# The first two contraction slices of a fused matmul–GELU–matmul, loaded and turned one at a time

## The chip, the core and the metric

The kernel runs on one core of one Trainium2 chip. The core has TensorE (PE in the profile; its weight loads are a row of their own, PEld), VectorE (DVE), ScalarE (ACT), GpSimd (POOL) and SyncE (SP), and 16 DMA engines that move data between the chip's main memory and the core's own. The metric is the device time of one execution in microseconds (us): the median over executions without the profiler.

## What is computed

```python
def setup_inputs():
    m, k, n, p = 1024, 1024, 2048, 1024
    return {
        "a": np.random.randn(m, k).astype(np.float32),
        "b": np.random.randn(k, n).astype(np.float32),
        "c": np.random.randn(n, p).astype(np.float32),
    }

def reference(a, b, c):
    h = np.matmul(a, b)
    h = 0.5 * h * (1 + np.tanh(np.sqrt(2 / np.pi) * (h + 0.044715 * h ** 3)))
    return np.matmul(h, c).astype(np.float32)
```

All inputs and the output are fp32 in main memory.

## The kernel before

The first product contracts over k = 1024, that is over eight slices of 128 (KT = 8). TensorE takes the contraction along the partitions, so b's slices can be used as they lie, while a must be turned: each 128 x 128 piece of a is cast to bf16, transposed on TensorE into PSUM (L145), and copied by VectorE into `aT` (L146). `aT[:, h, k]` holds slice k of row half h, where h = 0 stands for rows 0 to 511 of a and h = 1 for rows 512 to 1023.

**Stage 1** (L229 to L287) computes the first 512 columns of a·b in the plain way, in bf16. The output lies turned: column tile t (128 columns, t = 0 to 3) by row half h, each in a PSUM bank of its own `ps[h, t]`, summed over the eight slices by `block(h, tiles, ks)`, which issues one 128x128 by 128x512 matmul for each tile and slice (L114). GELU on ScalarE moves a finished bank to `hT` (L118).

**Later stages** compute the other 1536 columns of a·b and then the product with c by seven products in place of eight (class `Seven`, function `seven`; all their matmuls are at L212). VectorE makes the sums and differences that they need. They use the right half of b (`b1[:, :, 512:]`, `b2`) and `c_sb`. The change doesn't touch them.

**The loads have two routes.**

- *Plain loads* on SyncE's queue bring fp32 as it is. They go to `sta` (a) and `stb` (b), and VectorE or ScalarE cast them to bf16 (L110, L108). L75 to L79 issue, in this order: a's rows h = 0, columns 0 to 255 (512 KB); b's slices 0 and 1 of the left 512 columns (512 KB); a's h = 1, columns 0 to 255 (512 KB); a's h = 0, columns 256 to 511 (512 KB); b's slice 2 (256 KB).
- *Casting loads* on GpSimd's queue write bf16 straight into `abq`, `b1`, `b2` and `c_sb`. A part `a_part(h, q)` of a is 512 rows by 256 columns, two slices, 512 KB; q runs from 0 to 3. L91 and L92 issue a's (1, 1) and b's slice 3. The loop at L93 then issues for q = 2 and 3: a's (0, q), b's slices 2q and 2q+1, a's (1, q). Behind these follow the right half of b (L98, L101) and c (L104).

The casting queue is held back by `gate` (L81), a copy on GpSimd that reads one column of a's first plain load: GpSimd issues no casting load before that load has landed.

**The order of the work** is written out by hand. Each engine runs its own instructions in the order of the program, and waits at each for what it needs. TensorE's order in stage 1 is the text of L229 to L285. `stir` puts in small matmuls on a constant, which keep TensorE busy while it waits for the first data. `turn(h, q, i, ab)` is a generator: each `next` transposes one slice of part (h, q), four pieces, into a PSUM bank i and copies it out; from L255 on it takes its input straight from `abq`. `cast_a(h, q, ...)` casts a part with the engines named, `cast_b(k, ...)` a slice of b.

The banks matter in one place: tile t of row half 1 uses bank 4 + t, for t = 0 to 2 (L246), and the transposes of the casting parts use bank 7.

Of the kernel before, what the change touches and what calls it, by code (L numbers as in the profile page):

```python
# [9 lines left out]
F32 = mybir.dt.float32  # L10
F32R = mybir.dt.float32r
BF16 = mybir.dt.bfloat16
# [7 lines left out]
def kernel(ctx, tc, a, b, c, out):  # L20
    nc = tc.nc
    M, K = a.shape
    _, N = b.shape
    _, P = c.shape
    H = 512
# [3 lines left out]
    av = a.rearrange("(mt p) k -> p mt k", p=128)  # L29
    bv = b.rearrange("(kt p) n -> p kt n", p=128)  # L30
# [9 lines left out]
    def slot(tag, shape, dt, name):  # L40
        return big.tile(shape, dt, name=name, tag=tag)

    def bank(i, shape=(128, H), dt=F32, name="ps"):
        return pp.tile(list(shape), dt, name=name, tag=f"bank{i}", padded_shape=None)

    def pieces(tag, bufs, shape, dt, name):
        return small.tile(shape, dt, name=name, tag=tag, bufs=bufs)

    warm = nc.const_aps.tensor(0.0, [128, 256], F32)
    ident = consts.tile([128, 128], BF16, name="ident")  # L50
    make_identity(nc, ident)
    gate = consts.tile([128, 1], F32, name="gate")
# [6 lines left out]
    aT = slot("a", [128, 2, KT, H], BF16, "aT")  # L59
    b1 = slot("b1", [128, KT, 1024], BF16, "b1")  # L60
# [2 lines left out]

    KH = KT // 2
    stb = slot("x0", [128, KT, H], F32, "stb")
    sta = slot("x1", [128, 2, 2, 4, 256], F32, "sta")
    abq = slot("x3", [128, 4, 2, 4, 256], BF16, "abq")

    def a_part(h, q):
        return av[:, 4 * h:4 * h + 4, ds(q * 256, 256)]  # L70

    def b_part(q):
        return bv[:, 2 * q:2 * q + 2, 0:H]

    nc.sync.dma_start(out=sta[:, 0, 0], in_=a_part(0, 0))  # L75
    nc.sync.dma_start(out=stb[:, 0:2], in_=b_part(0))
    nc.sync.dma_start(out=sta[:, 1, 0], in_=a_part(1, 0))
    nc.sync.dma_start(out=sta[:, 0, 1], in_=a_part(0, 1))
    nc.sync.dma_start(out=stb[:, 2], in_=bv[:, 2, 0:H])  # L79

    nc.gpsimd.tensor_copy(gate, sta[:, 0, 0, 3, 0:1])  # L81
    nc.scalar.activation(g, warm[:, 0:1], AF.Gelu_apprx_tanh)


    def cast_load_a(h, q):
        nc.gpsimd.dma_start(out=abq[:, q, h], in_=a_part(h, q))  # L86

    def cast_load_b(q):
        nc.gpsimd.dma_start(out=b1[:, 2 * q:2 * q + 2, 0:H], in_=b_part(q))  # L89

    cast_load_a(1, 1)  # L91
    nc.gpsimd.dma_start(out=b1[:, 3, 0:H], in_=bv[:, 3, 0:H])  # L92
    for q in range(2, 4):  # L93
# [5 lines left out]
    for n in range(2):  # L99
        for k in range(0, KT, 4):  # L100
            nc.gpsimd.dma_start(out=b2[:, k:k + 4, ts(n, H)],  # L101
                                in_=bv[:, k:k + 4, ds(1024 + n * H, H)])
# [3 lines left out]
    def copy(eng, dst, src):  # L106
        if eng is nc.scalar:
            nc.scalar.activation(dst, src, AF.Copy)  # L108
        else:
            nc.vector.tensor_copy(dst, src)  # L110

    def mm1(p, t, h, ks):
        for k in ks:
            nc.tensor.matmul(p, b1[:, k, ts(t, 128)], aT[:, h, k],  # L114
                             start=(k == 0), stop=(k == KT - 1))
# [6 lines left out]
    def stir(*widths):  # L122

        for w in widths:
            nc.tensor.matmul(ps[0, 3][:, 0:w], warm[:, 0:128], warm[:, 0:w],
                             start=True, stop=True, skip_group_check=True)

    def cast_a(h, q, *engs):

        ab = pieces("ab", 2, [128, 4, 256], BF16, "ab")  # L130
        for i, eng in enumerate(engs):
            w = 256 // len(engs)
            for j, e in enumerate(eng if isinstance(eng, tuple) else (eng,)):
                m = slice(2 * j, 2 * j + 2) if isinstance(eng, tuple) else slice(0, 4)
                copy(e, ab[:, m, ts(i, w)], sta[:, h, q][:, m, ts(i, w)])
        return ab

    def turn(h, q, i, ab):

        banks = i if isinstance(i, tuple) else (i,)  # L140
        pts = [bank(x, (128, 2, H), BF16, "pt") for x in banks]
        for n in range(2):
            pt = pts[n % len(pts)]
            for m in range(4):
                nc.tensor.transpose(pt[:, n, ts(m, 128)], ab[:, m, ts(n, 128)], ident)  # L145
            nc.vector.tensor_copy(aT[:, h, 2 * q + n], pt[:, n])  # L146
            yield

    def cast_b(k, *engs):
        c0 = 0  # L150
        for i, eng in enumerate(engs):
            w = (H - c0) if i == len(engs) - 1 else H // len(engs) // 128 * 128
            copy(eng, b1[:, k, ds(c0, w)], stb[:, k, ds(c0, w)])
            c0 += w

    def block(h, tiles, ks):
        for k in ks:
            for t in tiles:
                mm1(ps[h, t], t, h, (k,))
# [66 lines left out]
    zero = Seven(4, quarters(b1, H, 256), BB, [None] * 4, [None] * 4, 2)  # L226
    one = Seven(4, quarters(b2, 0, H), BB, [None] * 4, zero.t)

    stir(256, 256, 256, 256, 256)  # L229
    tn = turn(0, 0, 4, cast_a(0, 0, nc.vector))  # L230
    next(tn)
    stir(128)
    cast_b(0, nc.vector, nc.vector, nc.scalar)
    next(tn)
    stir(64)
    cast_b(1, nc.scalar)
    ab = cast_a(1, 0, nc.vector, nc.scalar)
    block(0, range(4), (0,))
    block(0, range(2), (1,))
    for _ in turn(1, 0, (7, 6), ab):  # L240
        pass
    block(0, range(2, 4), (1,))
    ab = cast_a(0, 1, (nc.scalar, nc.vector), nc.vector)
    cast_b(2, nc.scalar, nc.scalar)
    for t in range(3):
        ps[1, t] = bank(4 + t)  # L246
    zero.t[0], zero.t[1] = pair(2)
    block(1, range(3), (0,))
    tn = turn(0, 1, 7, ab)
    next(tn)  # L250
    block(1, range(3), (1,))
    next(tn)
# [1 line left out]
    for q in range(1, 3):  # L254
        k = 2 * q  # L255
        block(0, range(4), (k,))
        tn = turn(1, q, 7, abq[:, q, 1])
# [5 lines left out]
        tn = turn(0, q + 1, 7, abq[:, q + 1, 0])  # L263
# [10 lines left out]
    tn = turn(1, 3, 0, abq[:, 3, 1])  # L274
# [213 lines left out]
```

## Time and profile before

| | |
|---|---|
| time, median of 3 runs | 117.2 us (117.19 to 117.28) |
| the profiled execution's own time | 117.6 us |
| its span, first to last instruction | 115.8 us |
| PE busy | 110.7 us (96% of the span), 544 matmuls |
| DVE / ACT / POOL busy | 90.1 / 51.4 / 17.3 us |
| granted TensorE clock | 1.00 throughout |
| first matmul of stage 1 on real data | 6.90 us |
| read from main memory, written to it | 20.97 MB, 4.19 MB |
| casting queue: packets, MB written | 8672, 9.31 |

The page divides the span into 40 slices of 2.9 us. PE's row is nearly full from the third slice on; the first two hold the stirring matmuls and the first transposes. The DMA row is full to the nineteenth slice, with 200 to 213 GB/s from the fifth on: a casting load is counted by the bf16 bytes that it writes, half of the fp32 bytes that it reads.

The loads have these rows: line, tile, queue, number, size of one, and the median time from the issue to the landing.

```profile
sta<-in_a_dram SPq DMA_DIRECT2D x3, 512.0 KB, 6.2
abq<-in_a_dram POOLq DMA_DIRECT2D x5, 256.0 KB, 8.0
stb<-in_b_dram SPq DMA_DIRECT2D x1, 512.0 KB, 5.4
b<-in_b_dram POOLq DMA_DIRECT2D x2, 256.0 KB, 8.3
stb<-in_b_dram SPq DMA_DIRECT2D x1, 256.0 KB, 7.2
```

In a timeline or chain, a row gives the start, the duration, the engine and line, and what is written from what; the bracket behind it gives the idle time of the engine before it and what ended that. In a table by stretches of time, each engine has its busy time and its number of instructions, and the last three columns are PE's clock, the DMA engines' busy share (which can exceed 1, as packets overlap) and the GB/s moved.

### The profile page before, as it was taken

The page shows a single profiled execution, that of the slowest core. Times are in us where ns is not written, and L with a number is a line of the kernel's source. Part 1 is how long each engine was busy: PE and PEld are TensorE (multiplying, and loading weights), DVE is VectorE, ACT ScalarE, POOL GpSimd, SP SyncE. Part 2 cuts the span into 40 slices and gives each one's busy share as a digit, 9 for nine tenths or more (in the row PEclk, how much of TensorE's full clock was granted, in tenths as well). Part 3 has the DMA queues.
Part 4 walks back from the last instruction along what each step waited for, and adds up shares of the span by engine and source line. Part 5 has one row for each costly group of instructions (what it writes and reads, how often), then busy time and mean ns, then how long its engine had stood idle before and what let it go on. Part 6 is the DMA issues. An engine that isn't in the chain of part 4 may idle for free.

```text
span 115.8 us, 1473 instructions
## 1 busy us (share of the span) xinstructions
PE 110.7 (96%) x544; PEld 77.1 (67%) x550; DVE 90.1 (78%) x108; ACT 51.4 (44%) x86; POOL 17.3 (15%) x29
## 2 busy tenths in 40 slices
PE   7889999999999999999999999999999999999990
PEld 6545555445777447888886444588888888888870
DVE  0247747689999998944789999999999986964581
ACT  5053000799268998066699339700043992000000
POOL 2497754222332000000000000000000000000000
PEclk9999999999999999999999999999999999999999
DMA  3999999999999999998000000070000002004994
GB/s 74 296 381 221 200 199 204 204 207 207 205 210 210 211 212 212 212 210 163 9 0 0 6 0 0 0 272 0 0 0 0 0 0 94 2 27 173 364 358 166
DMA packets 13414, 15.94 MB, mean 138 GB/s; under 512 B 736, under 2 KB 9184, under 8 KB 13408
## 3 DMA queue, kind: packets, MB, share of 16 engines
q0 software_dynamic: 8672, 9.31, 47.6%
q1 hardware_dynamic: 4592, 6.42, 15.7%
q10 hardware_dynamic: 144, 0.13, 0.3%
q8 instruction: 4, 0.07, 0.2%
q14 instruction: 2, 0.02, 0.0%
HBM read 20.97 MB, written 4.19 MB: 217 GB/s over the span
## 4 chain that ended last, share of the span: by engine, by line
PE 79%; DMA 13%; POOL 5%; issue 0%; DVE 0%
PE ps L212 76%; DMA abq<-in_a_dram 10%; DMA sta<-in_a_dram 3%; POOL abq L86 3%; PE ps L114 2%; POOL b L89 1%; POOL gate L81 1%; PE pt L145 1%; POOL b L92 0%; DVE ot L375 0%
## 5 line engine op out<-in xcount | busy, mean ns | idle before, releaser
L212 PE MATMUL ps<-x,s 128*128 128x512 f32 x128 | 29.6, 391 | 0.0
L212 PEld LDWEIGHTS ps<-x,s 128*128 128x128 f32 x128 | 24.0, 188 | 5.1
L212 PE MATMUL ps<-x,x 128*128 128x512 f32 x96 | 22.9, 394 | 0.0
L212 PEld LDWEIGHTS ps<-x,x 128*128 128x128 f32 x96 | 18.0, 188 | 3.9
L114 PE MATMUL ps<-aT,b 128*128 128x512 bf16 x62 | 15.7, 379 | 0.3 <-DVE b L110 0.2
L298 ACT ACTIVATE v<-ps 128x512 f32<-128x512 f32 x10 | 6.0, 598 | 19.1 <-PE ps L212 19.1
L212 PE MATMUL ps<-c_sb,hT 128*128 128x512 bf16 (+2 forms) x78 | 14.1, 336 | 0.1
L212 PE MATMUL ps<-x 128*128 128x512 f32 x56 | 13.2, 393 | 0.0
L212 PEld LDWEIGHTS ps<-x 128*128 128x128 f32 x56 | 10.2, 188 | 2.7 <-ACT u L298 0.4
L212 PEld LDWEIGHTS <-hT 128*128 128x128 bf16 x80 | 7.1, 98 | 7.0 <-issue 0.5
L118 ACT ACTIVATE hT<-ps 128x512 bf16<-128x512 f32 x14 | 7.3, 596 | 9.6 <-PE ps L114 9.6
L118 ACT ACTIVATE hT<-ot 128x512 bf16<-128x512 f32 x18 | 10.4, 623 | 2.1 <-DVE ot L303 2.0
L146 DVE COPY aT<-pt 128x512 bf16<-128x512 bf16 x16 | 6.7, 422 | 5.5 <-PE pt L145 5.4
L212 PE MATMUL ps<-aT,b 128*128 128x512 bf16 x46 | 10.6, 379 | 0.1
L303 DVE TENSOR_TENSOR ot<-ps,u 128x512 f32<-128x512 f32 x10 | 6.7, 688 | 5.2 <-ACT u L298 5.2
L303 DVE TENSOR_TENSOR ot<-ps,v 128x512 f32<-128x512 f32 x10 | 6.7, 688 | 4.9 <-DMA out_dram<-ot 3.9
L170 DVE TENSOR_TENSOR x<-c_sb 128x1024 fp32r<-128x1024 bf16 x8 | 9.2, 1216 | 0.0
L114 PEld LDWEIGHTS <-b 128*128 128x128 bf16 x64 | 5.7, 97 | 4.5 <-DVE b L110 0.3
L212 PEld LDWEIGHTS <-b 128*128 128x128 bf16 x48 | 4.6, 97 | 5.7 <-issue 0.3
L104 POOL DMA_DIRECT2D c_sb<-in_c_dram x8 | 5.6, 703 | 13.4 <-DMA b<-in_b_dram 11.1
L170 DVE TENSOR_TENSOR x<-b 128x1024 fp32r<-128x1024 bf16 (+1 forms) x4 | 7.0, 1751 | 0.6 <-issue 0.6
L298 ACT ACTIVATE u<-ps 128x512 f32<-128x512 f32 x10 | 5.9, 597 | 3.4 <-PE ps L212 3.2
(44 smaller groups left out, 110.7 us busy)
## 6 DMA issues: line engine op xcount, KB each, us to landing
c_sb<-in_c_dram POOLq DMA_DIRECT2D x8, 512.0 KB, 19.7
out_dram<-ot SPq DMA_DIRECT2D x14, 256.0 KB, 2.1
b<-in_b_dram POOLq DMA_DIRECT2D x6, 512.0 KB, 15.6
sta<-in_a_dram SPq DMA_DIRECT2D x3, 512.0 KB, 6.2
abq<-in_a_dram POOLq DMA_DIRECT2D x5, 256.0 KB, 8.0
stb<-in_b_dram SPq DMA_DIRECT2D x1, 512.0 KB, 5.4
b<-in_b_dram POOLq DMA_DIRECT2D x2, 256.0 KB, 8.3
stb<-in_b_dram SPq DMA_DIRECT2D x1, 256.0 KB, 7.2
```

Source lines behind the costliest of these rows:

```text
L81: nc.gpsimd.tensor_copy(gate, sta[:, 0, 0, 3, 0:1])
L86: nc.gpsimd.dma_start(out=abq[:, q, h], in_=a_part(h, q))
L89: nc.gpsimd.dma_start(out=b1[:, 2 * q:2 * q + 2, 0:H], in_=b_part(q))
L104: nc.gpsimd.dma_start(out=c_sb[:, t:t + 2], in_=cv[:, t:t + 2])
L114: nc.tensor.matmul(p, b1[:, k, ts(t, 128)], aT[:, h, k], start=(k == 0), stop=(k == KT - 1))
L118: nc.scalar.activation(hT[h][:, t], p, AF.Gelu_apprx_tanh)
L145: nc.tensor.transpose(pt[:, n, ts(m, 128)], ab[:, m, ts(n, 128)], ident)
L146: nc.vector.tensor_copy(aT[:, h, 2 * q + n], pt[:, n])
L170: nc.vector.tensor_tensor(out=dst[:, r], in0=x[:, r], in1=y[:, r], op=op)
L212: nc.tensor.matmul(p[:, ds(c0, w)], l[:, k, ts(j, 128)], r[:, k, ds(c0, w)], start=(start and k == 0), stop=(k == self.kt - 1), skip_group ...
L298: nc.scalar.activation(st, p, AF.Copy)
L303: nc.vector.tensor_tensor(out=ot, in0=p, in1=st, op=ADD)
```

## The change

The first two slices of a now come as four plain loads of one slice and one row half each (128 columns, 256 KB, in pieces of 512 bytes instead of 1 KB), and b's slices 0 and 1 as two loads of 256 KB. b's slice 0 is issued on ScalarE's queue, the other five on SyncE's. a's part (0, 1), which is slices 2 and 3 of row half 0, and b's slice 2 move from the plain loads to the head of the casting queue. The gate reads the first, now smaller, load of a. The casts and turns of the first two slices follow the new loads: each slice and row half is cast in two pieces of 128x256, turned by `turn_one` into bank 6 (slice 0) or 7 (slice 1), and copied out by `keep_one`.

```diff
-    sta = slot("x1", [128, 2, 2, 4, 256], F32, "sta")
+    sta = slot("x1", [128, 8, 4, 128], F32, "sta")
...
-    nc.sync.dma_start(out=sta[:, 0, 0], in_=a_part(0, 0))
-    nc.sync.dma_start(out=stb[:, 0:2], in_=b_part(0))
-    nc.sync.dma_start(out=sta[:, 1, 0], in_=a_part(1, 0))
-    nc.sync.dma_start(out=sta[:, 0, 1], in_=a_part(0, 1))
-    nc.sync.dma_start(out=stb[:, 2], in_=bv[:, 2, 0:H])
-
-    nc.gpsimd.tensor_copy(gate, sta[:, 0, 0, 3, 0:1])
+    def load_a(h, k):
+        nc.sync.dma_start(out=sta[:, 2 * k + h], in_=av[:, 4 * h:4 * h + 4, ts(k, 128)])
+
+    def load_b(eng, k):
+        eng.dma_start(out=stb[:, k], in_=bv[:, k, 0:H])
+
+    load_a(0, 0)
+    load_b(nc.scalar, 0)
+    load_a(1, 0)
+    load_a(0, 1)
+    load_b(nc.sync, 1)
+    load_a(1, 1)
+
+    nc.gpsimd.tensor_copy(gate, sta[:, 0, 3, 0:1])
...
+    cast_load_a(0, 1)
+    nc.gpsimd.dma_start(out=b1[:, 2, 0:H], in_=bv[:, 2, 0:H])
     cast_load_a(1, 1)
...
-    def cast_a(h, q, *engs):
...
+    def cast_a(h, k, *parts):
+
+        m0 = 0
+        for eng, m in parts:
+            r = slice(m0, m0 + m)
+            copy(eng, ab[k][:, h, r], sta[:, 2 * k + h][:, r])
+            m0 += m
+
+    def turn_one(h, k):
+        for m in range(4):
+            nc.tensor.transpose(pt[k][:, h, ts(m, 128)], ab[k][:, h, m], ident)
+
+    def keep_one(h, k):
+        nc.vector.tensor_copy(aT[:, h, k], pt[k][:, h])
...
-    stir(256, 256, 256, 256, 256)
-    tn = turn(0, 0, 4, cast_a(0, 0, nc.vector))
-    next(tn)
+    ab = [pieces("ab", 2, [128, 2, 4, 128], BF16, "ab") for k in range(2)]
+    pt = [bank(6 + k, (128, 2, H), BF16, "pt") for k in range(2)]
+    stir(256, 256, 256, 256, 128)
+    cast_a(0, 0, (nc.vector, 2), (nc.vector, 2))
+    turn_one(0, 0)
+    keep_one(0, 0)
     stir(128)
-    cast_b(0, nc.vector, nc.vector, nc.scalar)
-    next(tn)
+    cast_b(0, nc.scalar, nc.scalar)
     stir(64)
-    cast_b(1, nc.scalar)
-    ab = cast_a(1, 0, nc.vector, nc.scalar)
-    block(0, range(4), (0,))
-    block(0, range(2), (1,))
-    for _ in turn(1, 0, (7, 6), ab):
-        pass
-    block(0, range(2, 4), (1,))
-    ab = cast_a(0, 1, (nc.scalar, nc.vector), nc.vector)
-    cast_b(2, nc.scalar, nc.scalar)
+    cast_a(1, 0, (nc.vector, 2), (nc.scalar, 2))
+    cast_a(0, 1, (nc.vector, 2), (nc.scalar, 2))
+    block(0, range(2), (0,))
+    turn_one(1, 0)
+    keep_one(1, 0)
+    block(0, range(2, 4), (0,))
+    turn_one(0, 1)
+    keep_one(0, 1)
+    cast_b(1, nc.scalar, nc.scalar)
+    cast_a(1, 1, (nc.vector, 2), (nc.scalar, 2))
     for t in range(3):
         ps[1, t] = bank(4 + t)
     zero.t[0], zero.t[1] = pair(2)
     block(1, range(3), (0,))
-    tn = turn(0, 1, 7, ab)
+    block(0, range(2), (1,))
+    turn_one(1, 1)
+    keep_one(1, 1)
+    block(0, range(2, 4), (1,))
+    tn = turn(0, 1, 7, abq[:, 1, 0])
     next(tn)
     block(1, range(3), (1,))
     next(tn)
```

More of the change, by code (lines that the diff above doesn't have):

```diff
@@ L126, in stir @@
                              start=True, stop=True, skip_group_check=True)
-    def cast_a(h, q, *engs):
[L130 to L136, printed above, removed]
+    def cast_a(h, k, *parts):
[9 more added lines that the diff above has]
+        nc.vector.tensor_copy(aT[:, h, k], pt[k][:, h])
     def turn(h, q, i, ab):
```

## The prediction

> **What bounds the kernel now.** I read the chain of waits first. TensorE (PE) sets three quarters of it, and what stands before its long run is one transfer:
>
> ```profile
> 10.15 11.43 DMA abq<-in_a_dram
> 21.58 0.05 issue
> 21.63 0.40 PE pt L145 x4
> 22.02 0.65 PE ps L114 x3
> ```
>
> The last casting load of a (rows 512 to 1023, columns 768 to 1023; "a(1,3)" below) lands at 21.58 us; PE turns it at 21.63, and from there the chain is PE to the end. So the end is this landing plus 94.2 us (115.8 - 21.6). The PE timeline shows how near PE itself is to that:
>
> ```profile
> 10.03 0.39 PE L145 MATMUL pt<-ident,ab 128*128 128x128 bf16 x4
> ...
> 16.02 0.39 PE L145 MATMUL pt<-ident,abq 128*128 128x128 bf16 x4
> ...
> 19.16 2.32 PE L114 MATMUL ps<-aT,b 128*128 128x512 bf16 x10
> 21.63 0.40 PE L145 MATMUL pt<-ident,abq 128*128 128x128 bf16 x4
> ```
>
> The ten matmuls end at 21.48, so PE stands still for only 0.15 us before 21.63. It also met a load at 16.02: a(1,2) landed at 15.95. Between 10.03 and there it is busy. So PE and the stream of loads are level, and a gain needs both to come earlier. Then the table by stage (last two columns: busy share of the DMA engines, and GB/s moved; the casting queue writes half of what it reads):
>
> ```profile
> 2.00:2.50 0.50, 0.50 (x2) 0.41 (x2) 0.00 (x0) 0.23 (x2) 0.00 (x0) 1.00 0.94 123
> 2.50:4.00 1.50, 1.50 (x5) 1.15 (x5) 0.00 (x0) 0.00 (x0) 0.00 (x0) 1.00 1.07 350
> 4.00:5.50 1.50, 1.07 (x9) 0.65 (x7) 0.69 (x1) 0.00 (x0) 1.01 (x2) 1.00 0.93 253
> 5.50:6.50 1.00, 0.76 (x10) 0.59 (x8) 0.42 (x1) 0.00 (x0) 1.00 (x2) 1.00 1.04 341
> 6.50:8.50 2.00, 1.73 (x10) 0.70 (x9) 1.12 (x4) 1.45 (x3) 2.00 (x4) 1.00 1.09 389
> 8.50:9.50 1.00, 1.00 (x11) 0.73 (x12) 0.59 (x2) 0.14 (x2) 1.00 (x3) 1.00 1.10 298
> 9.50:11.00 1.50, 1.50 (x13) 0.76 (x11) 1.38 (x4) 1.12 (x3) 1.48 (x3) 1.00 1.40 201
> 11.00:19.00 8.00, 7.90 (x61) 4.44 (x62) 5.01 (x11) 0.00 (x0) 4.54 (x7) 1.00 1.37 199
> ```
>
> The transfers are never idle. SyncE's plain loads run until about 9; then the casting queue, at 199 to 201 GB/s written, 400 read. The issues show how long the casting loads stood waiting:
>
> ```profile
> 0.74 0.42 SPq L75 DMA_DIRECT2D sta<-in_a_dram  x1
> ...
> 2.82 0.71 SPq L79 DMA_DIRECT2D stb<-in_b_dram  x1
> 4.46 0.69 DVE L110 CAST ab<-sta 128x1024 bf16<-128x1024 f32 x1 [4.46 <-DMA sta<-in_a_dram]
> 4.49 0.70 POOL L81 COPY gate<-sta 128x1 f32<-128x1 f32 x1 [3.19 <-DMA sta<-in_a_dram]
> 5.14 0.88 POOL L86 DMA_DIRECT2D abq<-in_a_dram  x1
> ```
>
> Issued at 5.14, the first casting packet moves at 8.82 in the trace's packet records, as the plain loads run dry on one DMA engine after another (8.5 to 9.5).
>
> **The change, part by part.** 6 MB of fp32 still go before the end of a(1,3); only their route changes. So I ask by how much a(1,3) moves.
>
> (1) Plain loads shrink from 2.25 to 1.5 MB. Before, each of 16 DMA engines moves 96 pieces of 1 KB (a) and 24 of 2 KB (b). At 389 GB/s a 1 KB piece goes every 42 ns; a 2 KB packet takes 84 ns. That is 4.0 + 2.0 = 6.0 us. After: 128 pieces of 512 B and 16 of 2 KB (1.34 us). No load with 512 B pieces is in the trace. Bounds: 21 ns (the byte pace of 1 KB), so 2.7 us; or 42 ns (a whole piece's time), 5.4 us. Nearest row: the last stores' 512 B packets take 27 ns where 1 KB load packets take 46, so 42 x 27/46 = 25 ns, 3.2 us. I take that: 4.5 us, 1.5 less.
>
> (2) The casting queue gets 768 KB in front: 0.39 MB written at 201 GB/s, +1.96 us. With (1), the stream's end moves by +0.46 (bounds 0 and +2.7).
>
> The Trainium skill ("DMA: Bandwidth & Descriptors", section "Why small descriptors are slow (HBM only)") gives each packet a fixed cost of some 3 cycles beside one per 32 B, so 19 for 512 B against 35 for 1 KB; by that ratio of 0.54 instead of the rows' 0.59 the pieces would take 2.9 us and (1) and (2) together would come to +0.2. The rows are dearer than the page, and they stand.
>
> (3) The dip at 4.0 to 5.5 (253 GB/s where 350 and 389 stand around it) falls where b's first load begins, with single packets of 300 to 500 ns. It costs 1.5 x (1 - 253/370) = 0.47 us. With b's slice 0 on ScalarE's queue beside a's first load, this start lies beside a's own slow start (123 GB/s). Worth 0 to 0.47; I take 0.25, as nothing shows two queues starting together.
>
> (4) Does the casting queue follow at once? The gate (L81) waits for a's first load, now 256 KB, but b's slice 0 shares the DMA engines, so it lands between 3.7 (its bytes alone) and 4.45 (after both). Casting issues begin at 4.4 to 5.15, and the plain loads run dry from about 7.0 (8.5 - 1.5). If the casting queue only waits its turn, nothing is lost; if it is never ready sooner than 3.68 us after its issue (8.82 - 5.14), up to 1.8 are. The SW packets begin one DMA engine after another, some 0.25 us after each is done with plain ones, which speaks for waiting its turn. I take 0.1.
>
> The Trainium skill (the same page, section "Queues, rings and completion order") has each DMA engine go round the queues that have work, packet by packet. The rows at 6.5 to 8.5 hold 389 GB/s, with four casting issues done by 8.0 and no casting packet in them; by the rule those would have shared from about 7, and the queue was then not ready until 8.8, which is the dear end of (4) and rival A's time in place of the forecast's.
>
> (5) Issues. SyncE's five stay five, done by some 3.5. ScalarE issues one ahead of its table load (1.28 us): 0.4 to 0.7 by SyncE's rows, 0.38 by its own later row; it then idles until 4.4, so this is covered. GpSimd has two more in front (0.88 and 0.55), so a(1,1) is issued at 6.6 instead of 5.14, seconds of queue ahead of its bytes. Eight casting loads are out at once (the ninth, L98, waited for the first). a(1,3) becomes the tenth and waits for the second, about 10.2; it is issued near 12, and its bytes moved from 17.8 on. Covered.
>
> (6) PE's start. a's first load at 4.4, two DVE casts (128x256, 0.28 each), four transposes, copy (0.42): first real matmul at 5.7 instead of 6.90, b's casts on ScalarE (2 x 0.42) ready at 5.3. Then it waits: DVE's copy of turn (1,0) is queued behind the cast of (0,1), which lands near 6.2, so rows 512 on have their first operand at 6.9. b's slice 1 lands near 6.9 and its casts end at 7.7, behind which ScalarE casts its half of (1,1). The turn of (1,1) ends near 8.5, and its copy must leave bank 7 (0.42 + latency, 9.0) before the first casting load (landing near 9.6) is turned there. Before, that turn stood at 10.03: PE is some 0.4 ahead. It loses this at a(1,2). Cost and gain: 0.
>
> (7) DVE's and ScalarE's casts are nearly the same elements; both idle over half of 4 to 9 us. 0.
>
> Sum: +0.46 - 0.25 + 0.1 = **+0.3 us**, passed on whole, since PE meets a(1,2) and a(1,3) with no slack worth the name. The profiled execution took 117.6 (span 115.8 + 1.8), 0.4 over the median of 117.2; I add to the median: **117.5**.
>
> **Rivals.** *A: the casting queue is late* (dear end of 4). For: no casting packet in 3.7 us after its issue. Against: the staggered start. The casting queue starts at 8.82 less 0 to 0.75 and carries 1.96 more, of which some 0.25 was shared before: +1.0 to +1.7, **118.5**.
>
> *B, the other side: the stream ends earlier and PE's early start is kept.* 512 B pieces at the byte pace (0) and the whole dip saved (-0.47), with no wait at the casting queue. For: 512 B writes of the cast loads already go at 400 GB/s read. Against: the 27 ns packets. It decides from the point where (1) to (4) sum below -0.2; PE's lead of 0.4 caps it: **116.8**.
>
> *C: nothing shows.* One 16 KB packet of the instruction queue, at 19.57 for 0.97 us, held up one DMA engine: fifteen of its sixteen parts of a(1,3) had landed by 19.92, the last came at 21.58. It caught that engine's last two pieces. If it falls just behind them, a(1,3) lands over 1 us sooner, PE's 0.15 at 21.48 goes, and with a stream some 0.2 late the time is **117.25**. For: a matter of 0.1 us. Against: PE's instructions and the stream move together.
>
> **How the numbers follow.** Forecast 0.52, A 0.19, B 0.17, C 0.12. Within 0.2% of 117.2 (0.23 us, about what a measurement of this kernel can tell from no change) lie C and 0.14 of the forecast, whose own range is 117.25 to 117.95. Faster 0.17, same 0.26, slower 0.57. The range is 116.9 to 118.6: it leaves out half of B and the dear part of A and of the 512 B pieces.
>
> **What would show it.** Step 1: plain loads at 300 to 340 GB/s from 2.5 on. 3: no dip at 4 to 5.5. 4: casting writes of 200 GB/s from 7.3, not 8.8, with no empty stretch. 6: first matmul near 5.7, first casting turn near 9.6. The sum: a(1,3) turned near 21.9, and the end 94.2 behind. I am wrong if it is turned before 21.4 or after 22.6, or if PE no longer waits for it.

## The result and the profile after

| | before | after |
|---|---|---|
| time, median | 117.21 us (117.19 to 117.28) | 121.06 us (120.75 to 121.27, 4 runs) |
| ratio to before, 95% interval | | 1.0325 (1.0302 to 1.0348) |
| the profiled execution's own time, its span | 117.6, 115.8 us | 121.27, 119.5 us |
| a's first load landed | 4.44 us | 6.64 us |
| first matmul on real data | 6.90 us | 8.26 us |
| first casting issue, first casting packet | 5.14, 8.82 us | 6.94, 8.53 us |
| b's slice 3 landed (casting queue) | 11.98 us | 15.61 us |
| end of stage 1 (last L114 / L123 matmul) | 24.87 us | 28.14 us |
| from there to the last PE instruction | 88.06 us | 88.03 us |

The change costs 3.85 us, forecast were 0.3. (An execution more than 1.5% above the fastest of its kernel counts as slow and is left out; that was one of two in the experiment e7 below.) Of the profiled executions' 3.67 us, 3.27 have arisen by the end of stage 1. PE's work behind it is the same to 0.03 us; the rest lies in the tail and in what surrounds the span. First the chain of waits of the changed kernel (start, length, what):

```profile
0.74 5.90 DMA sta<-in_a_dram
...
9.12 6.49 DMA b<-in_b_dram
15.61 0.05 issue
15.65 1.04 PE ps L123 x4
...
28.14 88.03 PE ps L226 x408
```

Before, the chain hung on one transfer until 21.58 us. Now it leaves the transfers at 15.61, and from there PE is busy without a break to the end. Two transfers are late: a's first load, out for 5.90 us (before 3.70), and b's slice 3. The issues that answer to those of before, and PE's rows at the same steps:

```profile
0.74 0.44 ACTq L79 DMA_DIRECT2D stb<-in_b_dram  x1
6.70 0.31 POOL L88 COPY gate<-sta 128x1 f32<-128x1 f32 x1 [5.39 <-DMA sta<-in_a_dram]
6.94 0.87 POOL L93 DMA_DIRECT2D abq<-in_a_dram  x1
```

```profile
7.02 0.60 PE L147 MATMUL pt<-ident,ab 128*128 128x128 bf16 x4 [2.60 <-POOL gate L88]
...
8.26 1.06 PE L123 MATMUL ps<-aT,b 128*128 128x512 bf16 x2
...
12.70 0.38 PE L159 MATMUL pt<-ident,abq 128*128 128x128 bf16 x4
...
15.65 1.04 PE L123 MATMUL ps<-aT,b 128*128 128x512 bf16 x4 [0.26 <-DMA b<-in_b_dram]
...
24.91 0.39 PE L159 MATMUL pt<-ident,abq 128*128 128x128 bf16 x4
```

PE has nothing to do for 2.60 us before its first transposes (the bracket names the gate's copy, but what they read is a's first load, cast by VectorE from 6.67 on); a(1,3) is turned at 24.91 in place of 21.63. At 15.65 PE waited for a load for only 0.26 us. The table by stage (last three columns: PE's clock, DMA share, GB/s):

```profile
2.50:4.00 1.50, 1.50 (x5) 1.21 (x5) 0.00 (x0) 0.20 (x1) 0.00 (x0) 1.00 0.83 174
4.00:5.50 1.50, 0.42 (x3) 0.20 (x2) 0.00 (x0) 0.00 (x0) 0.00 (x0) 1.00 1.08 254
...
6.50:8.50 2.00, 1.48 (x9) 1.31 (x10) 1.34 (x5) 1.04 (x4) 1.80 (x4) 0.66 0.76 246
8.50:9.50 1.00, 1.00 (x6) 0.53 (x5) 0.01 (x1) 0.78 (x3) 1.00 (x2) 0.50 0.93 130
9.50:11.00 1.50, 1.50 (x11) 0.83 (x9) 0.53 (x2) 0.49 (x2) 1.50 (x3) 0.65 1.36 149
11.00:19.00 8.00, 7.51 (x54) 3.83 (x53) 4.39 (x11) 0.00 (x0) 5.80 (x9) 1.00 1.17 160
```

Three things are to be seen. The transfers start at half the rate (174 GB/s where before had 350). PE's clock is halved around 8.5 to 9.5 us, behind the 2.60 us without work. And the casting queue is slow, 160 GB/s from 11 to 19 where before had 199. In half microseconds it is plainer, 37 to 59 GB/s between 11 and 13:

```profile
11.00:11.50 0.50, 0.50 (x4) 0.21 (x3) 0.50 (x2) 0.00 (x0) 0.50 (x2) 1.00 0.64 58
11.50:12.00 0.50, 0.50 (x7) 0.29 (x5) 0.02 (x1) 0.00 (x0) 0.50 (x2) 1.00 0.52 43
12.00:12.50 0.50, 0.50 (x6) 0.23 (x4) 0.27 (x1) 0.00 (x0) 0.50 (x1) 1.00 0.54 37
12.50:13.00 0.50, 0.42 (x6) 0.29 (x5) 0.15 (x1) 0.00 (x0) 0.50 (x2) 1.00 0.51 59
```

The DMA engines are busy for only about half of that time (0.51 to 0.64, where the steady stream has 1.37): packets are slow, and between them the engines stand empty.

**The same 3.27 us, read twice.** *On PE:* from its first real matmul to the end of stage 1 it is busy for 19.39 of 19.88 us (before 17.61 of 17.97). So the delay is 1.36 from the later start, 1.78 from more busy time and 0.13 from more waiting. Of the 1.78, the half clock makes 1.15: 0.24 us of work at 0.5 before 8.5, 1.0 at 0.50, 1.5 at 0.65 add up to 0.12 + 0.50 + 0.53. The other 0.6 is not taken apart; a turn of four transposes that before stood ahead of the first matmul is in it. *On the loads:* by the mean over the 16 DMA engines, the last plain load lands at 8.30 (before 9.51). The four casting loads behind it then follow at gaps of 2.57, 1.48, 2.25 and 0.64 us, where a load of a takes 1.32 and one slice of b 0.66 in the steady stream. So b's slice 3 is late by −1.21 (plain loads) + 1.98 (two loads more on the queue) + 1.12 (its start: 2.57 − 1.32, less 0.13 that it took before) + 1.73 (slow packets: 0.82 + 0.93 − 0.02) = 3.62 us. Both accounts give the whole delay: two delays ran side by side, and the experiments had to part them.

The record of the four executions already says which one matters less. A stretch of half clock of 3.41 us, as the profiled one had, makes a mean clock of 0.986 over the span, and that is what it shows. The other three had 0.995 to 0.999, too much to hold such a stretch, and still took 120.75 to 121.10 us against its 121.27.

### The profile page after: what moved, and what is told of

Same layout as the page of the kernel before. It is cut to its first block, busy times and chain, and to the rows that moved or that the text cites. A ratio compares the mean times of both kernels' runs of the same rounds, so it can differ in the third digit from the quotient of the medians.

```text
span 119.5 us, 1481 instructions
## 1 busy us (share of the span) xinstructions
PE 112.3 (94%) x550; PEld 77.9 (65%) x550; DVE 89.1 (75%) x107; ACT 51.4 (43%) x87; POOL 18.2 (15%) x31
## 4 chain that ended last, share of the span: by engine, by line
PE 84%; DMA 10%; POOL 2%; DVE 0%; issue 0%
PE ps L226 74%; PE ps L123 8%; DMA b<-in_b_dram 5%; DMA sta<-in_a_dram 5%; PE pt L159 2%; POOL abq L93 1%; POOL b L99 0%; POOL gate L88 0%; DVE ot L396 0%
## 5 line engine op out<-in xcount | busy, mean ns | idle before, releaser
L123 PE MATMUL ps<-aT,b 128*128 128x512 bf16 x64 | 17.4, 395 | 0.3 <-DMA b<-in_b_dram 0.3
L226 PE MATMUL ps<-aT,b 128*128 128x512 bf16 x48 | 10.7, 379 | 0.0
L160 DVE COPY aT<-pt 128x512 bf16<-128x512 bf16 x12 | 5.1, 424 | 5.6 <-PE pt L159 5.6
L123 PEld LDWEIGHTS <-b 128*128 128x128 bf16 x64 | 5.9, 103 | 4.2 <-DMA b<-in_b_dram 0.4
```

Source lines behind the costliest of these rows:

```text
L123: nc.tensor.matmul(p, b1[:, k, ts(t, 128)], aT[:, h, k], start=(k == 0), stop=(k == KT - 1))
L226: nc.tensor.matmul(p[:, ds(c0, w)], l[:, k, ts(j, 128)], r[:, k, ds(c0, w)], start=(start and k == 0), stop=(k == self.kt - 1), skip_group ...
```

## The experiments

The same rows of a trace are read for each: when a's first load, b's slice 0 and b's slice 3 land, and how long single packets take. A 2 KB packet of a plain load of b usually takes 84 ns, a casting load's 98 ns for b and 60 ns for a. "Crawl" is a stretch in which packets of b take hundreds. Packets of a among them can be slow as well. In the changed kernel b's slice 0 crawls at 3 to 5 us (up to 1024 ns), and b's slice 2, the second casting load, at 10.25 to 12.75 (up to 944 ns).

The theories by their letters: **S**, the casting queue alone is at fault. **Q**, b's slice 0 on ScalarE's queue beside a's first load is. **F**, rows of b crawl when they are first touched. **H**, the casting queue crawls after a stretch in which the DMA engines stood empty. **P**, b's slice 2 crawls for how it stands in the queue (descriptors that come just in time) or for its shape; **W**, it or any load of a single slice crawls by its shape. **L**, what counts is the lead, the time from the first casting issue to the first casting packet.

### Undoing one part at a time

*e1: b's slice 0 back on SyncE's queue.*

```diff
-    load_b(nc.scalar, 0)
+    load_b(nc.sync, 0)
```

> The changed kernel with one edit: b's slice 0 is issued on SyncE's queue, second in its order, instead of on ScalarE's. Theory Q (two queues: b's slice 0 beside a's first load delays that load from 4.4 to 6.6 us, and with it TensorE's start, its clock and the gate): the first load of a lands near 4.0, the first real matmul stands near 6, TensorE's clock does not fall to 0.5, and the time comes back to 117.2 to 118.2 us. Theory S (the casting queue is the cause: with 768 KB more it runs short of work at 10.5 to 12.75 us whatever comes before): the load that TensorE waits for at 15.6 (b's slice 3) still lands after 14.5, and the time stays above 119.5.

118.63 us, ratio 1.0123 (1.0086 to 1.0160), between the figures of Q and S. a's first load landed at 3.33, the clock stayed full, the casting queue was issued at 3.63 and b's slice 2 on it went at a flat 98 ns. So one word in the diff brings back 2.4 of the 3.85 us. But b's slice 0 still crawled, now on SyncE's queue (up to 1248 ns at 2.75 to 5.5), landed at 6.15, and the first matmul stood at 6.64:

```profile
6.64 0.61 PE L123 MATMUL ps<-aT,b 128*128 128x512 bf16 x2 [0.54 <-ACT b L117]
```

*e2: the move undone, b's slice 0 left on ScalarE's queue.*

```diff
+    st01 = sta[:, 4:6].rearrange("p a m c -> p (a m c)").rearrange("p (m c) -> p m c", m=4)
+    nc.sync.dma_start(out=st01, in_=a_part(0, 1))
+    load_b(nc.sync, 2)
...
-    cast_load_a(0, 1)
-    nc.gpsimd.dma_start(out=b1[:, 2, 0:H], in_=bv[:, 2, 0:H])
```

> The changed kernel with the move undone: a's part (0, 1) and b's slice 2 are plain loads again, last on SyncE's queue, cast by ScalarE and VectorE; b's slice 0 stays on ScalarE's queue. Theory Q: a's first load still lands near 6.6 us and TensorE still starts near 8.3 at half clock; the time is 118.5 to 120. Theory S: b's slice 3 lands near 12 as before the change, the late start is hidden by the loads that TensorE meets at 16 and 21.6, and the time is 117.0 to 118.

118.28 us, ratio 1.0093 (1.0064 to 1.0122). a's first load landed at 5.84, PE stood still for 1.32 us at full clock, b's slice 3 landed at 12.72. The casting queue didn't crawl although b's slice 0 lay on the second queue. Neither theory's figure was met.

*e3: both undone, only the loads of one slice stay.*

```diff
-    load_b(nc.scalar, 0)
+    load_b(nc.sync, 0)
...
+    nc.sync.dma_start(out=st01, in_=a_part(0, 1))
+    load_b(nc.sync, 2)
...
-    cast_load_a(0, 1)
-    nc.gpsimd.dma_start(out=b1[:, 2, 0:H], in_=bv[:, 2, 0:H])
```

> Both undone: all plain loads on SyncE's queue, none moved to the casting queue; what is left of the change are the loads and turns of one slice at a time. Theory Q and theory S both: 117.0 to 117.6 us, first real matmul near 5.7 to 6. If the 512-byte pieces themselves are slow, 118 or more.

121.24 us, ratio 1.0346 (1.0239 to 1.0453): both theories missed by over 3 us. Nothing crawled on the casting queue. But the gate opened at 3.3, the casting issues began at 3.60, and from about 8.75 to 11.5 casting packets went one to one with those of the plain loads that were still to come. a(0,1), plain, landed at 12.65 (before 9.37), and PE stood still for it:

```profile
13.14 0.40 PE L160 MATMUL pt<-ident,abq 128*128 128x128 bf16 x4 [2.52 <-ACT abq L118]
```

So a casting queue that opens too early is a cost as well.

*e4: the move alone, on the kernel before.*

```diff
-    nc.sync.dma_start(out=sta[:, 0, 1], in_=a_part(0, 1))
-    nc.sync.dma_start(out=stb[:, 2], in_=bv[:, 2, 0:H])
...
+    cast_load_a(0, 1)
+    nc.gpsimd.dma_start(out=b1[:, 2, 0:H], in_=bv[:, 2, 0:H])
...
-    tn = turn(0, 1, 7, ab)
+    tn = turn(0, 1, 7, abq[:, 1, 0])
```

> The kernel before, with the move alone: a's part (0, 1) and b's slice 2 go to the head of the casting queue, the other plain loads stay as they were (512 KB, SyncE). Theory Q: no start is late, so 117.0 to 117.8 us. Theory S: the casting queue runs short as in the changed kernel, b's slice 3 lands after 14.5, and the time is 119.5 to 121.

119.89 us, ratio 1.0231 (1.0195 to 1.0267). In the move alone, PE's row and two rows of the table by stage:

```profile
14.77 1.04 PE L114 MATMUL ps<-aT,b 128*128 128x512 bf16 x4 [1.06 <-DMA b<-in_b_dram]
```

```profile
8.50:9.50 1.00, 1.00 (x7) 0.30 (x4) 0.64 (x2) 0.00 (x0) 1.00 (x2) 1.00 0.89 97
9.50:11.00 1.50, 1.11 (x9) 0.56 (x9) 0.42 (x1) 0.00 (x0) 1.50 (x3) 1.00 1.02 103
```

The DMA engines move 97 to 103 GB/s, where before had 298 and 201, and their busy share is 0.89 to 1.02, where before had 1.10 and 1.40: single packets take long, and fewer are under way at once. This start of the kernel is that of before (a's first load at 4.10, full clock), so the move crawls by itself.

*e11: the second queue alone, on the kernel before.*

```diff
-    nc.sync.dma_start(out=stb[:, 0:2], in_=b_part(0))
+    nc.scalar.dma_start(out=stb[:, 0], in_=bv[:, 0, 0:H])
+    nc.sync.dma_start(out=stb[:, 1], in_=bv[:, 1, 0:H])
```

> The kernel before with b's first plain load split: slice 0 on ScalarE's queue, slice 1 second on SyncE's; a's loads stay at 512 KB in 1 KB pieces. Theory Q (b's slice 0 beside a's first load delays it): a's first load lands after 5.3 us instead of 4.4, and the time is 117.6 to 118.8. Against it (the 512-byte pieces are needed for the delay): it lands before 4.8, and the time is 117.0 to 117.5.

121.73 us (121.21 to 122.25), ratio 1.0339 (1.0129 to 1.0549). PE's first transposes with b's slice 0 on the second queue:

```profile
7.72 0.40 PE L146 MATMUL pt<-ident,ab 128*128 128x128 bf16 x4 [2.63 <-POOL gate L82]
```

With a's loads as before (1 KB pieces), a's first load landed at 6.95 in place of 4.44, b's packets took 145 to 226 ns at 2.5 to 5 (median of each half microsecond; the longest 596), PE stood still for 2.63 us and its clock fell to 0.50. So the late start doesn't need the pieces of 512 bytes. It is far above Q's figure. The casting queue, issued at 7.65, crawled too, but PE, slowed, hardly noticed: it waited for 0.11 us between 9.6 and 28.

The Trainium skill ("DMA: Bandwidth & Descriptors", section "Issuing engines are not separate DMA queues") has issues from several engines interleave on the same DMA engines and save only the time of issuing. The run shows more than that: the one issue moved to the other queue cost 4.4 us (121.73 against 117.35 on the same chip), because of what the two loads did to each other.

*e15: two queues at the start, but neither with b.*

```diff
-    nc.sync.dma_start(out=sta[:, 1, 0], in_=a_part(1, 0))
+    nc.scalar.dma_start(out=sta[:, 1, 0], in_=a_part(1, 0))
```

> The kernel before with a's second load (rows 512 to 1023, 1 KB pieces) on ScalarE's queue in place of SyncE's, so two queues start together and neither holds b. Theory Q1 (any second queue at the start slows both): a's packets climb over 100 ns, a's first load lands at 6.3 to 7.0, 120 to 122 us. Theory Q2 (only the first reads of b crawl, whatever the queue): a's packets stay between 42 and 90 ns, the first load lands at 4.8 to 5.9, as two loads share the bytes, b's first load crawls when it begins, 117.5 to 119 us.

119.16 us, ratio 1.0121 (1.0039 to 1.0203), just above Q2's figure. Both loads of a shared the engines one to one at 46 ns a packet, 359 to 382 GB/s from 2.5 to 5.5, and landed at 5.22 and 5.70. So two queues together are not slow; b's first packets are. The cost came from elsewhere: b's slice 3 on the casting queue crawled at 9.5 to 12 (up to 1091 ns), landed at 13.96, and PE waited 1.10 us for it.

### What makes the casting queue crawl

*e5, e8, e6: b's rows touched early* by small loads on ScalarE's queue: b's slice 2 in the move alone (e5) and in the changed kernel (e8), b's slices 0 and 1 in the kernel before (e6).

```diff
+    nc.scalar.dma_start(out=room[:, 0:16], in_=bv[:, 2, 0:16])
```

> The kernel before with the move alone (119.89 us in the run before this) and one more small load: 64 bytes of each of the 128 rows of b's slice 2, on ScalarE's queue at the start, into a spare tile. Theory F (the first reads of rows of b are slow for some 3 us after the first request, wherever they stand in a queue; a load that arrives at engines with other work hides it): b's slice 2 in the casting queue then goes at the usual 98 ns a packet, its last part lands before 10.2 us instead of 11.54, b's slice 3 by 13 instead of 14.7, and the time falls to 117.3 to 118.4. Theory P (the casting queue's second load is slow for how it stands in the queue: descriptors that come just in time, or the single-slice shape): nothing changes, 119.5 to 120.2.

> The changed kernel with the same small load of b's slice 2 on ScalarE's queue, behind b's slice 0. Theory F: b's slice 2 is fast in the casting queue, b's slice 3 lands near 13.8 instead of 15.6, and the time is 119.0 to 119.8 (the late first load of a stays). Theory P: 120.7 to 121.4.

> The kernel before, with small loads of 32 bytes of each row of b's slices 0 and 1 on ScalarE's queue at the start, ahead of all other work there. Theory F: the dip at 4.0 to 5.5 us (253 GB/s) is gone or smaller, b's first load lands before 6.2 us instead of 6.6; the time is 116.8 to 117.2. Theory P: the dip stays, and the time is 117.1 to 117.5, since the small packets cost a little.

120.34 us (e5, 1.0246), 121.06 (e8, 1.0307, 1.0228 to 1.0386) and 117.90 (e6, 1.0028, 1.0001 to 1.0055). b's slice 2 crawled as before, and the slow start of b at 4 to 5.5 us in the kernel before stayed: F falls (e6's time lies above the figures of both theories). e8 told something else. a's first load landed at 6.06 in it (in e2, with the same first loads as the changed kernel, at 5.84, so this time varies by itself), and PE kept its full clock. PE's rows in it:

```profile
6.43 0.49 PE L148 MATMUL pt<-ident,ab 128*128 128x128 bf16 x4 [1.47 <-POOL gate L89]
...
14.56 0.40 PE L160 MATMUL pt<-ident,abq 128*128 128x128 bf16 x4 [0.65 <-DMA abq<-in_a_dram]
15.31 1.04 PE L124 MATMUL ps<-aT,b 128*128 128x512 bf16 x4 [0.36 <-DMA b<-in_b_dram]
```

It began its real matmuls at 7.44, 0.8 earlier than the changed kernel and at full speed, then waited 2.05 us for loads between 8.26 and 27, and ended in the same time. So the late casting loads are enough for the whole delay, without the half clock and with a start only 0.54 later than before, as the late and slow PE is in e11.

*e7: a(1,1) ahead of b's slice 2 on the queue; e10: b's slices 2 and 3 as one load; both on the move alone.*

```diff
     cast_load_a(0, 1)
-    nc.gpsimd.dma_start(out=b1[:, 2, 0:H], in_=bv[:, 2, 0:H])
     cast_load_a(1, 1)
+    nc.gpsimd.dma_start(out=b1[:, 2, 0:H], in_=bv[:, 2, 0:H])
```

```diff
     cast_load_a(0, 1)
-    nc.gpsimd.dma_start(out=b1[:, 2, 0:H], in_=bv[:, 2, 0:H])
+    cast_load_b(1)
     cast_load_a(1, 1)
-    nc.gpsimd.dma_start(out=b1[:, 3, 0:H], in_=bv[:, 3, 0:H])
```

> The kernel before with the move alone, and a's part (1, 1) put ahead of b's slice 2 in the casting queue. Theory F: b's slice 2 is asked for 0.7 us later and moves 1.3 us later, so only part of its slow time is covered: 118.0 to 119.3 us. Theory P, if the single-slice shape is slow by itself: as slow as before it, 119.5 to 120.5. Theory P, if the second place in the queue is slow: a's part (1, 1) has the slow packets now.

> The kernel before with the move alone, but b's slices 2 and 3 come as one casting load of 512 KB, second in the queue. Theory H: the pair crawls like slice 2 alone did, its last part lands after 12.5, and the time is 119.3 to 121 us. Theory W: it goes at 98 ns a packet, and the time is 117.2 to 118.2.

e7: 121.26 us (one execution), above all its figures. The loads of a in front went at 60 ns, and whatever came of b behind them crawled (up to 1205 ns); PE stood still for 2.12 us, and its clock fell again:

```profile
13.60 1.49 PE L114 MATMUL ps<-aT,b 128*128 128x512 bf16 x3 [2.12 <-DMA b<-in_b_dram]
```

e10: 119.77 (119.13 to 120.41, ratio 0.9952 to 1.0393), inconclusive in time; the pair crawled in part, up to 434 ns. So b crawls in either shape and at the second or third place. a's casting packets were slow at times too: in the table below they make 0.17 of e7's excess of 1.32 and 0.30 of e10's 0.73.

*e9: the kernel before, its gate on a's second load.*

```diff
-    nc.gpsimd.tensor_copy(gate, sta[:, 0, 0, 3, 0:1])
+    nc.gpsimd.tensor_copy(gate, sta[:, 1, 0, 3, 0:1])
```

> The kernel before with one edit: the gate reads a's second plain load (row half 1, landing near 8.0 us) instead of the first, so that the casting queue is ready only when the plain loads have run dry. Theory H (after an idle start of the DMA engines the casting queue's first loads of b crawl, 200 to 900 ns a packet instead of 98, where a start behind plain loads, one engine at a time, does not): b's slice 3, second in that queue, has such packets and lands after 14.5 instead of 12; the time is 119 to 121 us. Theory W (the slow one is b's slice 2 as a single-slice casting load, wherever the queue starts): slice 3 goes at 98 ns and everything is only late by the idle time, 117.8 to 118.7.

119.99 us (1.0191, 1.0012 to 1.0371). Two rows of its table by stage:

```profile
9.50:11.00 1.50, 1.50 (x13) 0.84 (x12) 1.10 (x4) 1.05 (x3) 1.50 (x3) 1.00 0.74 83
11.00:13.00 2.00, 1.33 (x11) 0.59 (x9) 1.02 (x2) 0.00 (x0) 2.00 (x4) 1.00 1.15 135
```

No load was changed, only the time at which the casting loads were issued (8.31 in place of 5.14), and b's slice 3, flat at 98 ns before, crawled (up to 568 ns). W falls.

*e12: the move, with the moved plain loads kept though unread* (768 KB more are read): as e4, without its first two removed lines.

```diff
+    cast_load_a(0, 1)
+    nc.gpsimd.dma_start(out=b1[:, 2, 0:H], in_=bv[:, 2, 0:H])
```

> The kernel before with the move, and the two moved plain loads kept as well, though nothing reads them: the casting queue again starts behind plain loads that run until about 9 us, and carries 768 KB more. Theory H: b's slice 2 in the casting queue goes at 98 ns a packet, the stream is late by the 1.9 us of the added bytes alone, and the time is 118.3 to 119.3 us, less than the 119.9 of the move without them. Theory W: slice 2 crawls as it did, and the time is 120.5 to 122.

119.96 us (119.79 to 120.13), between the theories. Behind the longer plain stream, nearly all of b's slice 2 went at 98 ns (single packets up to 392). What the extra bytes cost hides the gain.

*e13: the move alone with an earlier gate*, on an 8 KB touch of a; *e14: the same gate on the kernel before.*

```diff
+    nc.scalar.dma_start(out=room, in_=av[:, 7, 0:16])
...
-    nc.gpsimd.tensor_copy(gate, sta[:, 0, 0, 3, 0:1])
+    nc.gpsimd.tensor_copy(gate, room[:, 0:1])
```

> The move alone (a(0,1) and b's slice 2 on the casting queue, gate and plain loads otherwise as before), but the gate waits for an 8 KB touch of a's last rows on ScalarE's queue, which should land near 2.5 to 3, so the casting loads are issued near 3 to 3.5 instead of 4.8 and no DMA engine is empty before their first packet. Theory H (the crawl is that of an idle start): b's slice 2 goes at about 98 ns a packet, a(1,1) lands at 11.3 to 12.5, 117.4 to 118.4 us. Rival W (the first slices of b on the casting queue crawl anyhow once plain loads are few): slice 2 climbs over 200 ns as in the move alone, a(1,1) lands at 13 or later, 119.3 to 120.5 us.

> The kernel before with the same early gate: the control for the touch and for casting loads that are issued while plain ones still have to come. If the casting queue only waits for plain loads that were issued ahead of it: 117.2 to 117.9 us, first casting packet near 8.8. If it goes in among them one to one, a(0,1) and b's slice 2 land late, over 119 us.

e13: 118.03 us (1.0056, 1.0027 to 1.0085): the earlier gate takes back 1.9 of the 2.65 us that the move alone costs. e14: 118.19 (1.0068, 1.0032 to 1.0105), above its first figure: there the casting packets went in among the plain loads, one to one from 8.5 to 9.5, and a(0,1) landed at 10.71.

H did not survive e15, where the casting queue followed the plain loads without an empty stretch and crawled all the same. What sorts all kernels is L. The table gives, in microseconds, the first casting issue, the first casting packet, their difference, and the packets' excess: for casting packets over 100 ns (a) or 140 ns (b) up to 25 us, their time beyond the usual 60 and 98 ns, summed and divided by the 16 engines. The time in which engines stood empty between packets is not in it, so it is less than the delay. The last two rows were run after the law was put.

| kernel | issue | first packet | lead | excess | median time |
|---|---|---|---|---|---|
| e8, changed, b touched | 6.36 | 7.94 | 1.58 | 1.36 | 121.06 |
| the changed kernel | 6.94 | 8.53 | 1.59 | 1.03 | 121.06 |
| e9, before, gate late | 8.31 | 9.90 | 1.59 | 0.97 | 119.99 |
| e4, move alone | 4.80 | 6.41 | 1.61 | 1.26 | 119.89 |
| e10, move, pair of slices | 5.05 | 6.71 | 1.66 | 0.73 | 119.77 |
| e7, move, other order | 5.21 | 6.99 | 1.78 | 1.32 | 121.26 |
| e5, move, b touched | 5.05 | 6.84 | 1.79 | 1.21 | 120.34 |
| e11, second queue alone | 7.65 | 9.73 | 2.08 | 1.06 | 121.73 |
| e13, move, gate early | 3.88 | 6.52 | 2.64 | 0.40 | 118.03 |
| e15, a on ScalarE's queue | 5.92 | 8.59 | 2.67 | 0.50 | 119.16 |
| e2, changed without the move | 6.14 | 9.56 | 3.42 | 0.03 | 118.28 |
| before | 5.14 | 8.82 | 3.68 | 0.13 | 117.21 |
| e12, move, plain loads kept | 5.14 | 8.98 | 3.84 | 0.22 | 119.96 |
| e1, changed, b's slice 0 on SyncE | 3.63 | 7.58 | 3.95 | 0.03 | 118.63 |
| e6, before, b touched | 5.04 | 9.02 | 3.98 | 0.03 | 117.90 |
| e3, changed, both undone | 3.60 | 8.22 | 4.62 | 0.02 | 121.24 |
| e14, before, gate early | 2.74 | 7.57 | 4.83 | 0.02 | 118.19 |
| e16, changed, gate early | 3.36 | 7.61 | 4.25 | 0.03 | 119.03 |
| e17, move, no gate | 1.42 | 5.98 | 4.56 | 0.04 | 118.83 |

*e16: the changed kernel with the early gate; e17: the move alone without a gate.*

```diff
+    nc.scalar.dma_start(out=room, in_=av[:, 7, 0:16])
     load_a(0, 0)
     load_b(nc.scalar, 0)
...
-    nc.gpsimd.tensor_copy(gate, sta[:, 0, 3, 0:1])
+    nc.gpsimd.tensor_copy(gate, room[:, 0:1])
```

```diff
-    nc.gpsimd.tensor_copy(gate, sta[:, 0, 0, 3, 0:1])
```

> The changed kernel with the gate on an 8 KB touch of a, which landed at 2.6 to 3.7 us in the two runs that had it, so the casting loads are issued some 3 to 4 us earlier than at 6.94. Theory L (what decides the crawl is the lead, from the first casting issue to the first casting packet: in the fifteen kernels so far 3.4 us or more go with at most 0.2 us of excess packet time on each DMA engine, 2.6 with 0.4 to 0.5, 1.6 to 2.1 with 0.7 to 1.4): lead over 3.4, excess under 0.3, b's slice 2 at 98 ns a packet, and what is left of the delay is that of b's slice 0 on ScalarE's queue: 119 to 120.2 us. Rival (the crawl comes with the other parts of the change): excess near 1, 120.6 to 121.3 us.

> The move alone without any gate: GpSimd issues its casting loads from about 1 us on. Theory L: lead over 3.4 us if the casting queue still starts behind the plain loads, excess under 0.2 (1.26 in the move alone, 0.40 with the early gate), 117.2 to 118.0 us; if its packets go in among the plain loads at once, a's first load lands later than 4.4 and the time is 118 to 119.5, still without a crawl of the casting queue. Rival H as first put (only an empty stretch ahead of the first packet makes it crawl): the same here, so this run tells the law's upper end rather than one theory from another; excess of 0.4 or more would be against both.

No crawl in either, as L has it. e16: 119.03 us (1.0146, 1.0116 to 1.0175), 2.0 less than the changed kernel. It doesn't part the two causes cleanly: the touch, issued ahead of b's slice 0, delays that load as well, so a's first load landed at 3.48 and the clock stayed full. What is left is b's slice 0, which crawled at 3 to 5.5 us (up to 1087 ns) and landed at 6.59:

```profile
7.08 0.61 PE L124 MATMUL ps<-aT,b 128*128 128x512 bf16 x2 [1.66 <-ACT b L118]
```

e17: 118.83 us (1.0126, 1.0107 to 1.0145). Its price is the sharing of e3 and e14: casting packets one to one with those of a's second load at 7 to 7.5, which landed at 9.43 (7.44 in the move alone).

**What follows.** Each part of the change shortens the lead by itself: b's slice 0 beside a's first load holds the gate back (6.64), and 768 KB less of plain loads bring the casting queue's turn forward (leads of 2.08 in e11 and 1.61 in e4). e9 changed the issue time alone, e13 that and an 8 KB touch, and both moved the crawl with it; e16 and e17 were foretold by it. So that much is shown. What in the lead counts is not: with it rises the number of casting loads whose issue has begun before the first packet moves (3 with leads up to 2.08, 4 with 2.64 and 2.67, 5 to 7 from 3.42 on), so descriptors that come just in time, as P had it, would fit as well. How long b's own first load waits from its issue to its first packet fits less well: 3.29 us in e7, which crawled by 1.32, but 3.13 and 3.17 in e13 and e15, which crawled by 0.40 and 0.50. Why a short lead makes b's packets slow, and why b's first reads crawl in the first microseconds on either queue, was not found. No kernel beat the one before.

## Why the prediction was wrong

The sign was right; the size was 0.3 against 3.85 us. What the prediction asked for, by how much a(1,3) moves, came to 3.53 us by the mean over the 16 engines (19.65 to 23.18) in place of 0.3. Two steps failed: (3) and (4) took b's slice 0 beside a's first load as a matter of shared bytes, and no term held that the first casting loads could be slow. Point by point:

**What bounds it.** That stage 1's delay would pass on whole held: 88.06 and 88.03 us of PE behind it. That a(1,3)'s landing sets the end did not hold. Its last part landed at 23.53 and it was turned at 24.91, PE being the bound from 15.65 on.

**(1) Plain loads, 1.5 us less.** The pieces came out near the forecast. One slice and row half, 32 pieces for each engine, followed the load before it at 0.74 to 0.78 us, 24 ns a piece; 25 had been assumed. A 1 KB piece took 43 by the same count (1.37 and 1.38 for 32), so the ratio is 0.56, between the two that were weighed, 0.54 and 0.59. But the last plain load landed only 1.21 us sooner by the mean over the engines, where (1) with (3) had −1.75. The missing 0.5 was lost at the start, in what (3) prices: a's first load and b's slice 0, 512 KB, had landed by 5.36 on the mean, where before the first 512 KB, all of a, had by 4.15.

**(2) The casting queue, +1.96.** The bytes cost that much at the steady gaps (1.98). The pace of 201 GB/s did not hold over the first loads: +1.73 of crawl that no term contained.

**(3) and (4), the steps that failed first.** The forecast had that "this start lies beside a's own slow start", worth 0 to 0.47, and that the gate's load "lands between 3.7 (its bytes alone) and 4.45 (after both)". It landed at 6.64. The step took two loads side by side as sharing bytes, which e15 shows for two loads of a. But b's first packets take hundreds of ns, and beside them a's load came no faster. The trace of before showed these packets (300 to 500 ns at 4 to 5.5 us) when nothing urgent stood behind them; they were priced by the bytes they lose there, and not as a delay of whatever shares the engines. The same rows beside the first load cost the gate 2.2 us, PE's start 1.36 and, in the profiled execution, its clock 1.15.

**(4), the casting queue's turn.** "If the casting queue only waits its turn, nothing is lost." It does wait its turn, and is ready 1.6 us after its issue when the engines are free (the changed kernel, e9), so the 3.68 us of before were waiting, as forecast. But nothing is lost only while it waits long. With a lead of 1.6 it costs 1.12 at its start and 1.73 behind.

The round-robin rule of the Trainium skill, weighed there ("DMA: Bandwidth & Descriptors", section "Queues, rings and completion order"), agrees with the runs only from 3.95 to 4.83 us after the first casting issue (e1, e3, e14, e16, e17), when packets of both queues go in turn. Before that the casting queue stayed out while plain loads ran, which the section does not tell.

**(5) Issues and (7) casts.** Covered, as said: GpSimd's two more issues stood ahead of nothing that was due.

**(6) PE's start**, 5.7 for the first matmul and 0.4 ahead of before at the first casting turn, built on (4): measured 8.26 and 12.70, where that turn stood at 10.03 before. The term was put at 0; by the account on PE it holds the whole 3.27 us.

**The rivals.** A had the casting queue late by up to 1.8 us; its readiness took 1.6, but the cost came from the crawl and from a's first load, which A did not hold. B had the dip of (3) saved; it grew. C's cause was real: the 16 KB packet came at 23.15, while the parts of a(1,3) were landing (23.00 to 23.53), and held up none of them; it no longer mattered. Of the signs of being wrong two came true: a(1,3) was turned after 22.6, and PE no longer waited for it.

## What to carry to other kernels

A load that shows single slow packets where nothing waits for it must not be put beside the load that everything waits for: price it by the slow packets' time as a delay of the neighbour, and not by the bytes lost. A queue whose turn comes later than its issue is not late but has a reserve; when work ahead of it is taken away or its gate is held back, look at the lead that is left, and in the other direction at what it will go in among. And where two delays run side by side, undo them together as well as singly: removing only the late clock here (e8) changed nothing.

## What was not expected of the hardware

- b's first reads crawl in the first microseconds on either queue (up to 1248 ns for a 2 KB packet that usually takes 84), a's mostly at their usual 46 or 27, with single ones up to 496 before the change and 836 after it; touching the same rows early doesn't help (e5, e6, e8).
- In these nineteen kernels a casting queue with a lead of 1.58 to 2.08 us from issue to first packet has an excess of 0.73 to 1.36 us on each DMA engine in its first loads, most of it in b's packets; with 2.64 and 2.67, 0.40 and 0.50; from 3.42 on, 0.02 to 0.22.
- PE's clock fell to 0.50 after 2.60, 2.63 and 2.12 us without work (the changed kernel, e11, e7) and stayed full after 1.66 (e16), but also after 2.52 (e3). The traces' clock records fit both: they change only at edges 3.41 us or a multiple of it apart. Where PE was without work for 2.12 to 2.64 us between two edges, the clock was 0.50 in the next stretch; where for 1.75 at most (e4), it stayed. e3's 2.52 us are cut by an edge at 12.05. The Trainium skill ("TensorE: Matmul & The Clock Gate", section "HAM oscillation — how this bites in real kernels") gives gaps over about 3.4 us as the point; here shorter ones sufficed in three kernels.
- SyncE's eighth issue took 2.18 us in e3 and its sixth 1.98 us in e2, where the others of these two took 0.43 to 0.69. What they waited for is not known.
